# The first weight sum of a seven-product pair: from a VectorE addition to a GpSimd transfer that adds on writing

## The chip, the cores and the metric

One core of a Trainium2 chip runs the whole program. The metric is the device time of one execution in microseconds (us). The kernel before takes 2045.4 us, the median of 2 runs (2044.98 to 2045.83).

The engines are named as in the profile: PE is TensorE (matmuls), DVE is VectorE, ACT is ScalarE, POOL is GpSimd, and SP is SyncE, whose queue issues nearly all transfers from memory.

## The reference

A block of a streaming encoder on 256 rows of width 4096, all in float32. Cut to the parts whose weights matter here:

```
xn   = rms_norm(x, norm_in_g)
proj = xn @ w_in                      # 4096 x 14336: q, k, v, z_a, a_c, g_c, z_c
y_a  = rms_norm(chunked_attention(q, k, v, rel_table)) * silu(z_a)
y_c  = rms_norm(conv_module(a_c, g_c, ..., w_pw)) * silu(z_c)
h    = x + concat(y_a, y_c) @ w_out   # 4096 x 4096
gate = sigmoid(rms_norm(h) @ w_ple_gate + b_ple_gate)   # 4096 x 4096
out  = rms_norm(h + gate * (p @ w_ple))
```

Nearly all of the time is the product of 256 rows with these weights, which are read once from memory, about 400 MB.

## The kernel before, in words

**Exact products from two parts.** A float32 weight block `wt` is split into a high part `wh` (a cast on ACT, type fp32r) and a low part `wl = wt - wh` (a subtraction on DVE, `minus`, line 321). The activations are split in the same way beforehand. One block product then costs three matmuls: high by high, low by high and high by low.

**Units.** The inner dimension is cut into blocks of 128 rows and the weight columns into blocks of 512. A unit takes one pair of row blocks (`k0 = 2*pair`, `k1 = k0 + 1`) and two column blocks that lie `apart` columns from each other. Its weights are two tiles of 128 x 2 x 512 (512 KB each): `w0` holds the two column blocks of `k0`, `w1` those of `k1`. With the two halves of the 256 rows, a unit is a 2 x 2 by 2 x 2 block product:

- A *pair* unit does it with eight block products: 24 matmuls. It needs 2 casts and 2 subtractions `minus`.
- A *seven* unit (marked with `*` in the orders of lines 266 to 270) does it with seven, by Strassen's and Winograd's scheme: 21 matmuls. It needs sums of the weights in place of one product: first `w0[:,1] = w0[:,1] + w1[:,1]` (`plus`, line 485), then `w0[:,0] = w0[:,1] - w0[:,0]` (`less`, line 486), then `w1 = w1 - w0[:,0]` (`less`, line 490). The first sum is that of the second column block of `k0` and the second column block of `k1`. `w0` and `w1` are also split before they are overwritten, and their sums are split after. On DVE that makes, in this order: `l0` (half a tile), the `plus`, the first `less`, `l1`, the second `less`, `al`, `bl`. On ACT the casts are `h0` (half a tile), `h1`, `ah` (line 488), `bh` (line 491).
- A *one* unit takes two row blocks of a single column block, 12 matmuls, with one tile.

`mixed_product` (line 430) runs 16 units of the kinds pair and seven in a given order; `product` (line 329) runs one units. There are 117 seven units: in the products of the convolution's gate and of q and k (orders `early`), in the four gate products (`delayed` once, then `dense`), in the four output products (`late`, then `dense`), and in three products with `w_ple_gate` (`late`, then `steady`). `dense` reads `1 0* 3 2* 5 4* 6* 7 8* 9 10* 11 12* 14* 13 15`: mostly pair and seven in turn, twice two sevens side by side.

**What sets the order.** The orders above are written out by hand. `prepare` (line 274) takes the next unit of the plan ahead of its use: it asks for its tiles in the pool `wpool` (`WB = 5` tiles of 512 KB for loads, and five buffers each for the high and the low parts), issues the loads from SP's queue and the first casts. In a seven unit, `prepare` for the next unit is called after the cast `bh`; its `al` and `bl` follow after it. `chain` (line 97) ties the splits and sums of each engine in the order in which they are written; other work is placed between them by the scheduler. A load has to wait until the last reader of the tile five places earlier is done. In a steady row of pair and seven in turn, the first tile `w0` of a seven unit takes the place of the second tile of the pair unit before last, which its `minus` frees; the second tile `w1` takes the place of the `w0` of the seven unit before, which `al` frees.

**Queues.** POOL does next to nothing before the change: a few fills, the power that makes a reciprocal root (line 148), four fills of the attention bias (line 919), and four operations at the end. No transfer is issued from it.

Of the kernel before, what the change touches and what calls it, by code (L numbers as in the profile page):

```python
# [13 lines left out]
ALU = mybir.AluOpType  # L14
# [3 lines left out]
NB = 512  # L18
# [13 lines left out]
def hybrid_block(  # L32
# [23 lines left out]
    nc = tc.nc  # L56
# [40 lines left out]
    def chain(ins):  # L97

        prev = last_of.get(ins.ins.engine)
        if prev is not None:  # L100
            tc.add_manual_dep(
                ins.ins, prev.name,
                mybir.DependencyInfo(mybir.DependencyClass.NoSync, mybir.DependencyReason.DATA),
                reason="order of the parts",
            )
        last_of[ins.ins.engine] = ins.ins
        return ins
# [101 lines left out]
    def fill(n):  # L209
        step()  # L210
        credit[0] += n
        while later and credit[0] > 0:
            item = later.popleft()
            weight, item = item if isinstance(item, tuple) else (1, item)
            credit[0] -= weight
            item()
        if not later:
            credit[0] = 0
# [11 lines left out]
    def part(tag):  # L230
        return wpool.tile([P, KC, NB], F32R, tag=tag, name=tag, bufs=HB)
# [42 lines left out]
    def prepare():  # L274

        if prepared or not plan:
            return
        unit = plan.popleft()
        w, col, apart, at, kind = unit
        wts, highs = [], []  # L280
        if kind == "one":
            wt = wpool.tile([P, KC, NB], F32, tag="w", name="wt")
            nc.sync.dma_start(
                wt,
                w[at * P : (at + KC) * P, col : col + NB].rearrange("(k q) n -> q k n", q=P),
            )
            wts.append(wt)
        else:
            for k in range(2):
                wt = wpool.tile([P, 2, NB], F32, tag="w", name="wt")  # L290
                kb = 2 * at + k
                rows = w[kb * P : (kb + 1) * P, :]
                nc.sync.dma_start(
                    wt,
                    bass.AP(
                        tensor=rows.tensor, offset=rows.offset + col,
                        ap=[list(rows.ap[0]), [apart, 2], [1, NB]],
                    ),
                )
                wts.append(wt)  # L300
        for k, wt in enumerate(wts):
            n = 1 if kind == "seven" and k == 0 else 2
            highs.append(part("wh"))
            chain(nc.scalar.copy(highs[k][:, :n], wt[:, :n]))  # L304
        prepared.append((unit, wts, highs))

    def take(*unit):

        prepare()
        found, wts, highs = prepared.pop()  # L310
        assert found[1:] == unit[1:] and found[0] is unit[0], (found, unit)
        return wts, highs
# [7 lines left out]
    def minus(wl, wt, wh):  # L320
        return chain(nc.vector.tensor_tensor(wl, wt, wh.bitcast(F32), ALU.subtract))  # L321

    def plus(out, a, b):
        return chain(nc.vector.tensor_tensor(out, a, b, ALU.add))  # L324

    def less(out, a, b):
        return chain(nc.vector.tensor_tensor(out, a, b, ALU.subtract))  # L327
# [102 lines left out]
    def mixed_product(  # L430
        w, col, lhs, comb, order, on_helpers, ahead=None, fills=0, on_begin=None, apart=NB
# [13 lines left out]
        def add(name, x, w2, n, final):  # L445

            for kind, (a, b) in enumerate(((x[0], w2[0]), (x[1], w2[0]), (x[0], w2[1]))):
                made.append(
                    nc.tensor.matmul(  # L449
                        banks[name], a, b, start=name not in begun,  # L450
                        stop=final and ends[name] == n and kind == 2,
                    )
                )
                begun.add(name)

        def block(kb, h):
            t = lhs[kb // 4]
            return [t[:, kb % 4, q, h * P : (h + 1) * P] for q in range(2)]

        last_seven = max((n for n, (_, seven) in enumerate(order) if seven), default=None)  # L460
        for n, (pair, seven) in enumerate(order):
            if ahead:
                ahead(pair)
            (w0, w1), (h0, h1) = take(w, col, apart, pair, "seven" if seven else "pair")
            l0, l1 = part("wl"), part("wl")
            if not seven:
                for wt, wh, wl in ((w0, h0, l0), (w1, h1, l1)):
                    minus(wl, wt, wh)
                prepare()
                fill(fills[0] if isinstance(fills, tuple) else fills)  # L470
                parts = ((h0, l0), (h1, l1))
                places = [(k, j, h) for k in range(2) for j in range(2) for h in range(NH)]
                if n in (0, len(order) - 1):
                    places = [(k, j, h) for j in range(2) for h in range(NH) for k in range(2)]
                for k, j, h in places:
                    name = (("P2", "P3"), ("P4", "X"))[h][j]
                    add(name, block(2 * pair + k, h), [t[:, j] for t in parts[k]], n, k == 1)
                continue
            begins = not helper
            if begins:  # L480
                for name in ("P1", "P5", "P7", "P6"):
                    helper[name] = ps_tmp.tile([P, NB], F32, tag="tmp", name=f"acc_{name}")
                banks.update(helper)
            minus(l0[:, :1], w0[:, :1], h0[:, :1])
            plus(w0[:, 1], w0[:, 1], w1[:, 1])
            less(w0[:, 0], w0[:, 1], w0[:, 0])
            ah, bh = part("wh"), part("wh")
            chain(nc.scalar.copy(ah, w0))  # L488
            minus(l1, w1, h1)
            less(w1, w1, w0[:, :1].to_broadcast([P, 2, NB]))  # L490
            chain(nc.scalar.copy(bh, w1))  # L491
            prepare()
            fill(fills[1] if isinstance(fills, tuple) else fills)
            al, bl = part("wl"), part("wl")
            minus(al, w0, ah)
            minus(bl, w1, bh)
            first = len(made)

            def s_of(i):
                t, at = comb[pair // 4], pair % 4  # L500
                return [t[:, at + i // 2, q, (i % 2) * P : (i % 2 + 1) * P] for q in range(2)]

            k0, k1 = 2 * pair, 2 * pair + 1
            add("P1", block(k0, 0), (h0[:, 0], l0[:, 0]), n, True)
            add("P2", block(k1, 0), (h1[:, 0], l1[:, 0]), n, True)
            add("P3", s_of(3), (h1[:, 1], l1[:, 1]), n, True)
            add("P6", s_of(2), (ah[:, 0], al[:, 0]), n, True)
            add("P7", s_of(0), (ah[:, 1], al[:, 1]), n, True)
            add("P5", s_of(1), (bh[:, 1], bl[:, 1]), n, True)
            add("P4", block(k1, 1), (bh[:, 0], bl[:, 0]), n, True)  # L510
            if begins and on_begin:
                on_begin()
            if begins:
                tc.add_manual_dep(
                    made[first].ins, last_transpose[0].ins.name,
                    mybir.DependencyInfo(mybir.DependencyClass.NoSync, mybir.DependencyReason.DATA),
                    reason="transposes before the helpers take their banks",
                )
            if n == last_seven:
                on_helpers(helper)  # L520
# [74 lines left out]
    def first_products():  # L595
# [21 lines left out]
        def add(k, parts, *kinds):  # L617
# [13 lines left out]
    rows = [(conv_ln_g, KCW), (conv_ln_b, KCW), (b_dw, KCW), (attn_out_g, AW // P),  # L631
            (conv_out_g, KCW), (ple_norm_g, KD)]
# [360 lines left out]
    for c in range(6):  # L993
        rows = spool.tile([P, 2, NB], F32, tag="stage", name="comb")
# [76 lines left out]
    for c0 in range(0, D // NB, 2):  # L1071
# [8 lines left out]
        def on_helpers(helper):  # L1080
            _, z = sum_tiles()
            h00, h01, h10, h11 = (hs[c0 + j][:, h, :] for h in range(NH) for j in range(2))
            tt(h00, helper["P1"], h00, ALU.add)
            helper_sums(helper, z)
            tt(h01, h01, z[0][1], ALU.add)
            tt(h10, h10, z[1][0], ALU.add)
            tt(h11, h11, z[1][1], ALU.add)
# [150 lines left out]
```

## Time and profile before

| | |
|---|---|
| time, median of 2 runs | 2045.4 us (2044.98 to 2045.83) |
| the profiled execution's own time | 2045.17 us |
| its span, first to last instruction | 2043.4 us |
| PE busy | 2018.3 us (99%), 9103 matmuls |
| DVE busy | 1801.0 us (88%) |
| ACT busy | 1373.3 us (67%) |
| POOL busy | 14.7 us (1%) |
| transfers | 412.29 MB, 202 GB/s over the span |
| granted TensorE clock | 0.996 |

Busy time is a mean over stages that differ: the profile's 40 slices show DVE between half busy (the last ones) and nine tenths or more (the gate, output and ple-gate products). The chain of waits follows the work back from the last instruction to what released it, so it says which engine's work set the end. A group row gives the summed busy time of instructions of one line and kind, the mean duration in ns, and after the bar the idle time of that engine just ahead of them. A timeline row starts with its start and its duration in us; a row with `x5` holds five instructions one after the other. SPq rows are issues of transfers, whose landing is a different row: the transfers' view gives the time from issue to landing.

### The profile page before, as it was taken

What the parts mean: (1) busy time and instruction counts of PE and PEld (TensorE: products, weight loads), DVE (VectorE), ACT (ScalarE), POOL (GpSimd) and SP (SyncE); (2) the same over time, 40 slices, a digit from 0 to 9 for tenths busy, and PEclk for the clock granted to TensorE, in tenths of its full rate; (3) what the DMA queues carried; (4) which work ended last, traced back from release to release, by engine and by line L of the source; (5) the groups of instructions that cost most, each with busy time, mean ns of one, the idle gap of its engine ahead of it and who ended that gap; (6) DMA issues with size and microseconds to landing.
All of it is one profiled execution on the core that took longest, in us unless ns stands there. A gap on an engine that the chain in (4) does not pass through costs nothing.

```text
span 2043.4 us, 26018 instructions
## 1 busy us (share of the span) xinstructions
PE 2018.3 (99%) x9103; PEld 1668.4 (82%) x9103; DVE 1801.0 (88%) x2124; ACT 1373.3 (67%) x2033; POOL 14.7 (1%) x23
## 2 busy tenths in 40 slices
PE   9999999999999999999999999999999999999997
PEld 6888888888888888878888888888888888888886
DVE  7589997999799988975889999999999998999954
ACT  7477798778977797774555656675565675665543
POOL 0000000000000000000000000000000000000010
PEclk9999999999999999999999999999999999999999
DMA  8646665666566665746565665666656655666774
GB/s 303 186 165 207 191 208 171 213 195 208 165 198 203 196 196 175 217 153 214 171 227 173 214 208 192 239 227 198 214 191 221 206 191 191 211 229 206 230 221 144
DMA packets 170333, 412.29 MB, mean 202 GB/s; under 512 B 13006, under 2 KB 16222, under 8 KB 170202
## 3 DMA queue, kind: packets, MB, share of 16 engines
q1 hardware_dynamic: 169914, 410.11, 62.1%
q8 instruction: 71, 1.16, 0.2%
q10 hardware_dynamic: 288, 0.52, 0.1%
q14 instruction: 60, 0.49, 0.1%
HBM read 406.39 MB, written 4.19 MB: 201 GB/s over the span
## 4 chain that ended last, share of the span: by engine, by line
PE 95%; DVE 2%; ACT 1%; issue 1%; DMA 1%; ACTq 0%; POOLq 0%; POOL 0%; DVEq 0%
PE acc L449 55%; PE acc L255 22%; PE acc_P L449 15%; DVE wl L321 1%; PE tmp_ps L179 1%; DMA wt<-in_w_in_dram 0%; PE tmp_ps L888 0%; PE tmp_ps L924 0%; PE tmp_ps L946 0%; ACT big_t L854 0%; ACT wh L304 0%; ACT junk L564 0%; PE tmp_ps L134 0%; DMA pin<-in_p_dram 0%; PE tmp_ps L923 0%
## 5 line engine op out<-in xcount | busy, mean ns | idle before, releaser
L321 DVE TENSOR_TENSOR wl<-wt,wh 128x1024 fp32r<-128x1024 f32 x961 | 1091.8, 1156 | 143.0 <-ACT wh L304 119.4
L449 PE MATMUL acc<-wh,big_t 128*128 128x512 f32 x3410 | 1052.2, 390 | 1.3 <-ACT big_t L165 0.7
L304 ACT CAST wh<-wt 128x1024 fp32r<-128x1024 f32 x727 | 698.5, 981 | 324.1 <-PE acc L449 106.1
L449 PEld LDWEIGHTS acc<-wh,big_t 128*128 128x128 f32 x3410 | 638.4, 188 | 133.5 <-ACT big_t L165 1.2
L449 PE MATMUL acc<-wl,big_t 128*128 128x512 f32 x1705 | 662.8, 389 | 0.4 <-DVE wl L321 0.4
L255 PE MATMUL acc<-wh,big_t 128*128 128x512 f32 x1248 | 393.8, 397 | 7.1 <-ACT wh L304 5.7
L449 PEld LDWEIGHTS acc<-wl,big_t 128*128 128x128 f32 x1705 | 320.0, 188 | 67.5 <-DVE wl L321 0.8
L255 PEld LDWEIGHTS acc<-wh,big_t 128*128 128x128 f32 x1248 | 232.5, 189 | 55.8 <-ACT wh L304 6.5
L449 PE MATMUL acc_P<-wh,big_t 128*128 128x512 f32 x852 | 262.2, 389 | 0.3 <-ACT wh L491 0.3
L255 PE MATMUL acc<-wl,big_t 128*128 128x512 f32 x624 | 244.1, 392 | 0.1
L327 DVE TENSOR_TENSOR wt<-wt 128x512 f32<-128x512 f32 x234 | 224.2, 958 | 7.5
L491 ACT CAST wh<-wt 128x1024 fp32r<-128x1024 f32 x117 | 123.3, 1054 | 158.1 <-DVE wt L327 129.2
L716 ACT ACTIVATE prod<-uT,dw 128x255 f32<-128x255 f32 (+14 forms) x480 | 200.7, 489 | 2.7 <-DVE cv L723 2.5
L449 PEld LDWEIGHTS acc_P<-wh,big_t 128*128 128x128 f32 x852 | 159.7, 188 | 33.6 <-ACT wh L491 0.7
L488 ACT CAST wh<-wt 128x1024 fp32r<-128x1024 f32 x117 | 123.3, 1054 | 81.5 <-DVE wt L327 76.4
L449 PE MATMUL acc_P<-wl,big_t 128*128 128x512 f32 x426 | 165.3, 389 | 0.0
L723 DVE TENSOR_TENSOR cv<-cv,prod 128x1020 f32<-128x1020 f32 (+14 forms) x120 | 138.7, 1156 | 21.2 <-ACT prod L716 21.0
L255 PEld LDWEIGHTS acc<-wl,big_t 128*128 128x128 f32 x624 | 117.5, 189 | 26.5 <-DVE wl L321 1.3
L449 PEld LDWEIGHTS acc_P<-wl,big_t 128*128 128x128 f32 x426 | 79.9, 188 | 17.0 <-DVE wl L321 0.2
L324 DVE TENSOR_TENSOR wt<-wt 128x512 f32<-128x512 f32 x117 | 80.2, 685 | 0.2 <-DMA wt<-in_w_ple_gate_dram 0.2
L564 ACT ACTIVATE junk<-hc 128x512 bf16<-128x512 f32 x32 | 20.2, 630 | 20.9 <-DVE hc L1095 8.4
L165 ACT ACTIVATE big_t<-tmp_ps,prm 128x256 fp32r<-128x256 f32 x64 | 27.5, 473 | 4.6 <-DVE big_t L166 4.6
(190 smaller groups left out, 937.9 us busy)
## 6 DMA issues: line engine op xcount, KB each, us to landing
wt<-in_w_in_dram SPq DMA_DIRECT2D x447, 512.0 KB, 4.6
wt<-in_w_out_dram SPq DMA_DIRECT2D x128, 512.0 KB, 4.6
wt<-in_w_ple_gate_dram SPq DMA_DIRECT2D x128, 512.0 KB, 4.4
wt<-in_w_pw_dram SPq DMA_DIRECT2D x32, 512.0 KB, 4.6
hc<-in_x_dram SPq DMA_DIRECT2D x8, 512.0 KB, 5.4
wt<-in_w_ple_dram SPq DMA_DIRECT2D x8, 512.0 KB, 5.5
out_dram<-hc SPq DMA_DIRECT2D x16, 256.0 KB, 2.7
xin<-in_x_dram SPq DMA_DIRECT2D x7, 512.0 KB, 8.0
```

Of the source, the lines that this page charges most:

```text
L165: nc.scalar.activation(hi, src, AF.Identity, scale=scale),
L179: nc.tensor.transpose(pt[:, i * T + h * P : i * T + (h + 1) * P], src[:, h, b * P : (b + 1) * P], ident,)
L255: nc.tensor.matmul(acc, a, b[:, k, :], start=kb == 0 and kind == 0, stop=kb == kblocks - 1 and kind == 2,)
L304: chain(nc.scalar.copy(highs[k][:, :n], wt[:, :n]))
L321: return chain(nc.vector.tensor_tensor(wl, wt, wh.bitcast(F32), ALU.subtract))
L324: return chain(nc.vector.tensor_tensor(out, a, b, ALU.add))
L327: return chain(nc.vector.tensor_tensor(out, a, b, ALU.subtract))
L449: nc.tensor.matmul(banks[name], a, b, start=name not in begun, stop=final and ends[name] == n and kind == 2,)
L488: chain(nc.scalar.copy(ah, w0))
L491: chain(nc.scalar.copy(bh, w1))
L716: chain(nc.scalar.activation(dst[:, i, : T - n], uT[:, i, : T - n], AF.Identity, scale=dw[:, b, TAPS - 1 - n : TAPS - n], bias=0.0 if n el ...
L723: chain(nc.vector.tensor_tensor(cv[:, :, n:], cv[:, :, n:], made[n][:, :, : T - n], ALU.add))
```

## The change

In `prepare`, the two loads of a seven unit are followed by a third transfer, of 256 KB: it is issued from POOL's queue, reads the second column block of `k1` from memory once more (`rows` still names `k1` after the loop), and adds it to the second half of `w0` on writing. `w0[:,1]` so becomes the sum that `plus` made, and the `plus` in `mixed_product` goes. Nothing else is edited. Lines from 301 on move down by 4, those after 485 by 3: `minus` is line 325, `less` line 331.

```diff
--- before.py
+++ after.py
@@ -298,6 +298,10 @@
                     ),
                 )
                 wts.append(wt)
+            if kind == "seven":
+                nc.gpsimd.dma_start(
+                    wts[0][:, 1, :], rows[:, col + apart : col + apart + NB], accum_op=ALU.add
+                )
         for k, wt in enumerate(wts):
             n = 1 if kind == "seven" and k == 0 else 2
             highs.append(part("wh"))
@@ -482,7 +486,6 @@
                     helper[name] = ps_tmp.tile([P, NB], F32, tag="tmp", name=f"acc_{name}")
                 banks.update(helper)
             minus(l0[:, :1], w0[:, :1], h0[:, :1])
-            plus(w0[:, 1], w0[:, 1], w1[:, 1])
             less(w0[:, 0], w0[:, 1], w0[:, 0])
             ah, bh = part("wh"), part("wh")
             chain(nc.scalar.copy(ah, w0))
```

In the rows below, the names in brackets are what the instruction waits for: `DMAHW` counts the landings of SP's transfers, `DMASW` those of POOL's, and an engine's name its own counter.

DVE before, a seven unit of the fourth gate product (its unit `2*`), with the pair unit ahead of it:

```order
1141 L321 TENSOR_TENSOR wl<-wt,wh 128x1024 [waits DMAHW0_49,PE_49,Activation_49]
1142 L321 TENSOR_TENSOR wl<-wt,wh 128x1024 [waits DMAHW1_49,PE_49,Activation_49]
1143 L321 TENSOR_TENSOR wl<-wt,wh 128x512 [waits DMAHW2_49,PE_49,Activation_49]
1144 L324 TENSOR_TENSOR wt<-wt 128x512 [waits DMAHW3_49]
1145 L327 TENSOR_TENSOR wt<-wt 128x512 [waits DVE_49]
1146 L321 TENSOR_TENSOR wl<-wt,wh 128x1024 [waits PE_49,Activation_49]
1147 L327 TENSOR_TENSOR wt<-wt 128x1024 [waits DVE_49]
```

and the same unit on DVE after the change:

```order
1077 L325 TENSOR_TENSOR wl<-wt,wh 128x1024 [waits DMAHW0_49,PE_49,Activation_49]
1078 L325 TENSOR_TENSOR wl<-wt,wh 128x1024 [waits DMAHW1_49,PE_49,Activation_49]
1079 L325 TENSOR_TENSOR wl<-wt,wh 128x512 [waits DMAHW2_49,PE_49,Activation_49]
1080 L331 TENSOR_TENSOR wt<-wt 128x512 [waits DMASW0_49,DVE_49]
1081 L325 TENSOR_TENSOR wl<-wt,wh 128x1024 [waits DMAHW3_49,PE_49,Activation_49]
1082 L331 TENSOR_TENSOR wt<-wt 128x1024 [waits DVE_49]
```

The `plus` of line 324, which waited for the landing of `w1` (`DMAHW3`), is gone; the first `less` stands in its place and waits for POOL's transfer; the landing of `w1` is now waited for by `l1` (and by the cast `h1` on ACT, as before).

DVE before, at the start of the same product (lines 1051 and 216 are the end of the product before: 1051 empties its accumulators):

```order
1126 L1051 TENSOR_TENSOR z<-acc_10170,z 128x512 [waits PE_49]
1127 L321 TENSOR_TENSOR wl<-wt,wh 128x512 [waits DMAHW6_49,Activation_49]
1128 L1051 TENSOR_TENSOR z<-acc_10172,z 128x512 [waits DVE_49,PE_49]
1129 L216 SCALAR_TENSOR_TENSOR y_c<-y_c,r_c,z 128x512 [waits Activation_49,Pool_49]
1130 L324 TENSOR_TENSOR wt<-wt 128x512 [waits DMAHW7_49]
1131 L1051 TENSOR_TENSOR z<-acc_10171,z 128x512 [waits PE_49]
1132 L216 SCALAR_TENSOR_TENSOR y_c<-y_c,r_c,z 128x512 [waits Activation_49]
1133 L1051 TENSOR_TENSOR z<-acc_10173,z 128x512 [waits PE_49]
1134 L327 TENSOR_TENSOR wt<-wt 128x512 [waits DVE_49]
```

and after the change (line 1054 is the former 1051):

```order
1063 L325 TENSOR_TENSOR wl<-wt,wh 128x512 [waits DMAHW6_49,PE_49,Activation_49]
1064 L1054 TENSOR_TENSOR z<-acc_10170,z 128x512 [waits PE_49]
1065 L331 TENSOR_TENSOR wt<-wt 128x512 [waits DMASW7_49,DVE_49]
1066 L1054 TENSOR_TENSOR z<-acc_10172,z 128x512 [waits PE_49]
1067 L216 SCALAR_TENSOR_TENSOR y_c<-y_c,r_c,z 128x512 [waits Activation_49,Pool_49]
1068 L1054 TENSOR_TENSOR z<-acc_10171,z 128x512 [waits PE_49]
```

Here the first `less` has moved up: it stood behind all four emptyings of accumulators and now stands ahead of three of them.

POOL after the change, around the first gate product (before, the fill of line 922, then line 919, and the powers of line 148 follow each other there):

```order
57 L922 MEMSET bias 64x4x64 [waits DVE_49,DMAHW7_49,PE_49,Pool_49]
58 L148 TENSOR_TENSOR r_ln<-r_ln,mhalf 128x2 [waits DVE_49]
59 L148 TENSOR_TENSOR r_a<-r_a,mhalf 128x2 [waits DVE_49]
60 L302 DMA wt<-in_w_in_dram 128x512 [waits DMAHW3_49,DMAHW4_49,DMAHW2_49,DMAHW5_49,DMAHW0_49,DMAHW7_49,DMASW1_49,DVE_49]
61 L148 TENSOR_TENSOR r_c<-r_c,mhalf 128x2 [waits DVE_49]
62 L302 DMA wt<-in_w_in_dram 128x512 [waits DMAHW1_49,DMAHW0_49,DMAHW3_49,DMASW5_49,DMAHW6_49,DVE_49,Activation_49]
```

The 117 transfers stand in one row on POOL, with its few other instructions between them. Of the landings that each waits for, the youngest is that of its own `w0`; the others belong to tiles of earlier units. On SP's queue the order differs only around some loads of `x` in the first output product and one load of a bias row.

## The prediction

> **What bounds the kernel now.** I read the page's busy times and chain first, then the waits of PE, then the chain and the DVE rows inside a single seven unit.
>
> ```profile
> span 2043.4 us, 26018 instructions
> PE 2018.3 (99%) x9103; PEld 1668.4 (82%) x9103; DVE 1801.0 (88%) x2124; ACT 1373.3 (67%) x2033; POOL 14.7 (1%) x23
> ```
>
> ```profile
> PE 95%; DVE 2%; ACT 1%; issue 1%; DMA 1%; ACTq 0%; POOLq 0%; POOL 0%; DVEq 0%
> ```
>
> The first lines give the span and each engine's busy time, the last the chain's shares. PE is busy for 2018.3 of 2043.4 us and is 95% of the chain. What an engine beside it saves can come back only where PE waits for it, and PE's longest waits are these (us in total, times, longest):
>
> ```profile
> PE acc L255 <- ACT wh L304: 5.7, 2, 4.5
> ...
> PE acc L449 <- DVE wl L321: 0.4, 1, 0.4
> PE acc_P L449 <- ACT wh L491: 0.3, 1, 0.3
> ```
>
> Only the last two belong to seven units (line 449): 0.7 us. The 5.7 us belong to one units (line 255), which the change leaves alone. So the gain is at most about 0.7 us, and the question is what the new transfer can cost. For that the fourth gate product is read, first on the chain, in which the run of nine `acc_P` marks a seven unit:
>
> ```profile
> 1270.57 2.04 PE acc_P L449 x9
> ...
> 1275.33 2.04 PE acc_P L449 x9
> ...
> 1285.53 2.04 PE acc_P L449 x9
> ```
>
> PE runs without a gap: a pair and a seven in turn take 1285.53 - 1275.33 = 10.20 us (45 matmuls), two sevens side by side 1275.33 - 1270.57 = 4.76 us. These three runs are the units `4*`, `6*` and `8*`. DVE, for `6*`, `8*` and `10*`:
>
> ```profile
> 1269.65 0.69 DVE L324 TENSOR_TENSOR wt<-wt 128x512 f32<-128x512 f32 x1
> ...
> 1273.38 1.22 DVE L321 TENSOR_TENSOR wl<-wt,wh 128x1024 fp32r<-128x1024 f32 x1
> ...
> 1278.67 0.68 DVE L324 TENSOR_TENSOR wt<-wt 128x512 f32<-128x512 f32 x1
> 1279.39 0.69 DVE L327 TENSOR_TENSOR wt<-wt 128x512 f32<-128x512 f32 x1
> 1280.00 1.22 DVE L321 TENSOR_TENSOR wl<-wt,wh 128x1024 fp32r<-128x1024 f32 x1
> 1281.25 1.23 DVE L327 TENSOR_TENSOR wt<-wt 128x1024 f32<-128x1024 f32 x1
> 1282.39 2.50 DVE L321 TENSOR_TENSOR wl<-wt,wh 128x1024 fp32r<-128x1024 f32 x2
> ...
> 1287.69 0.69 DVE L324 TENSOR_TENSOR wt<-wt 128x512 f32<-128x512 f32 x1
> ```
>
> DVE needs 1287.69 - 1278.67 = 9.02 us for a pair and a seven, so it regains 10.20 - 9.02 = 1.18 us on PE in each. A seven alone costs it the half subtraction `l0`, 0.6, and 1278.67 to 1282.39 + 2.50, 6.2: 6.8 us, where PE, side by side with another seven, needs 4.76. So it uses up its lead there: `al` of `6*` ends at 1273.38 + 1.22 = 1274.60, and PE's run that reads it starts at 1275.33. DVE is less than 1 us ahead then, and a delay that returned with every seven unit would reach PE.
>
> **What is removed.** One `plus` per seven unit:
>
> ```profile
> L324 DVE TENSOR_TENSOR wt<-wt 128x512 f32<-128x512 f32 x117 | 80.2, 685 | 0.2 <-DMA wt<-in_w_ple_gate_dram 0.2
> ```
>
> 117 x 0.685 = 80.2 us of DVE; with its spacing in the rows above (1278.67 to 1279.39) 0.72 us per unit. On the path it is worth at most the 0.7 us of PE's waits. What takes its place as DVE's last wait is `l1`, which needs the cast `h1`, which needs `w1`:
>
> ```profile
> 1274.62 0.33 SPq L293 DMA_DIRECT2D wt<-in_w_in_dram  x1
> wt<-in_w_in_dram SPq DMA_DIRECT2D x1, 512.0 KB, 3.8
> 1278.57 1.05 ACT L304 CAST wh<-wt 128x1024 fp32r<-128x1024 f32 x1 [1.54 <-DMA wt<-in_w_in_dram]
> ```
>
> The load of `8*`'s `w1` goes out when `al` of `6*` ends, lands 3.8 us later, and is cast until 1279.62; `l1` starts at 1280.00. Without the `plus`, `l1` moves forward by 0.38 us, not by 0.72.
>
> **What is added.** A chain: `w0` lands, POOL issues, 256 KB are read and added, the first `less` starts. POOL's queue is idle and the other landings that it waits for are older, so the chain starts at the landing of `w0`. How long it may last without moving `less` is the time from there to the `plus` of today. Two units, each with the issue of `w0`, its time to landing, and its `plus` (that of `10*` is above):
>
> ```profile
> 1278.18 0.33 SPq L293 DMA_DIRECT2D wt<-in_w_in_dram  x1
> wt<-in_w_in_dram SPq DMA_DIRECT2D x1, 512.0 KB, 5.6
> 455.48 0.37 SPq L293 DMA_DIRECT2D wt<-in_w_in_dram  x1
> wt<-in_w_in_dram SPq DMA_DIRECT2D x1, 512.0 KB, 5.8
> 467.21 0.69 DVE L324 TENSOR_TENSOR wt<-wt 128x512 f32<-128x512 f32 x1
> ```
>
> `10*`: 1278.18 + 5.6 = 1283.8, and 1287.69 - 1283.8 leaves 3.9 us. In an `early` product: 455.48 + 5.8 = 461.3, and 467.21 leaves 5.9 us. Each has 0.7 us more before DVE is later than today, since the `plus` is gone.
>
> The transfer itself, from POOL's issue to its landing, is not in this trace; no row has a transfer that adds, nor one issued from POOL. The nearest are the plain ones of 256 KB that SP issues among the weight loads, and the shortest (one of 256 KB) and longest landing of any weight tile:
>
> ```profile
> row<-in_b_ple_gate_dram SPq DMA_DIRECT2D x8, 256.0 KB, 4.9
> DMA to landing us min/median/max: 3.0/4.6/9.7
> ```
>
> So it lies between 3.0 and 9.7 us. I take 5.0: it runs among weight loads as the 4.9 us row does, and it reads as many bytes as a 512 KB load (256 KB from memory, 256 KB of the old values), which takes 4.6. With 5.0 us the early products hide it (5.9), and `10*` starts `less` at 1288.8 instead of 1288.41, a delay of 0.4 us that the next pair regains.
>
> The Trainium skill ("DMA: Bandwidth & Descriptors", section "Anatomy of one DMA — SWDGE (gpsimd) path") fits transfers from GpSimd by 2.0 us plus bytes over 436 GB/s; worked out for 256 KB that is an estimate of 2.6 us, by which all units hide it and the sum would be 2045 us. It names no price for the adding, and no run here shows one yet.
>
> **The load beside it.** The new transfer moves its data while `w1` is under way, and `w1` is what DVE waits for next. The engines' share of one load:
>
> ```profile
> q1 hardware_dynamic: 169914, 410.11, 62.1%
> ```
>
> 0.621 x 2043.4 us for 410.11 MB is 1.62 us for a 512 KB tile on all 16 engines, 0.81 us for 256 KB. A `w1` that shares the engines lands later by 0.8 us, or 1.6 if the old values cost as much as the new ones; below nothing it can't go, as nothing is removed from any queue. From one issue of `w1` to the next, today: 3.8 + 0.1 + 1.05 (cast), then `l1`, `less`, `al` from 1280.00 to 1283.61, 3.6 us: 8.6 us. It becomes 9.4 to 10.2, against DVE's 9.02 of today and PE's 10.20. In turns DVE keeps up, but regains only 0 to 0.8 us. A `dense` product has two sevens that follow a seven; each costs 6.8 - 4.76 = 2.0 us of lead today, 1.3 without the `plus`, 2.6 us per product, to be regained in five turns. I take 1.0 us of delay, nearer to the plain transfer's: five turns give 5 x 0.6 = 3.0, nothing is lost. At 1.6 us nothing is regained, and the six `dense` products (three of the gate, three of the output) lose 6 x 2.6 = 16 us.
>
> **Product starts.** In `dense` and `steady` products `less` now stands ahead of three emptyings of the last product's accumulators. If it waits, PE's banks wait. There the room is small:
>
> ```profile
> 1232.22 0.33 SPq L293 DMA_DIRECT2D wt<-in_w_in_dram  x1
> wt<-in_w_in_dram SPq DMA_DIRECT2D x1, 512.0 KB, 5.2
> 1240.24 0.69 DVE L1051 TENSOR_TENSOR z<-acc,z 128x512 f32<-128x512 f32 x1
> ```
>
> `w0` lands at 1237.4, the sum at 1242.4, and the emptying of 1240.24 comes 2.2 us late. It is the second bank of four; PE fills the first for six matmuls, 6 x 10.20 / 45 = 1.4 us, before it needs the next. That is between nothing and 0.8 us for each of eight starts, up to 6 us; I take 2. POOL's `r_c` now queues behind a transfer, but it is wanted only in the third gate product.
>
> **Sum.** The profiled execution took 2045.17 us for its span of 2043.4, 0.2 below the median. 2045.2 - 0.7 + 2 = 2046.5, with the median's 0.2 us 2046.7; I forecast 2047.
>
> **The rivals.** *The sum comes late* (slower). If adding costs more than I take, `less` waits in every seven unit. This feeds back: the split of pair unit 7, ahead of `8*`, frees the place for the `w0` of `10*`, and two turns later the split of pair unit 11, behind `10*`, frees that of another seven. In between lie 5.6 us of load, the transfer, and DVE's work from a `less` to the end of the next pair's split, 1279.39 to 1287.69 less the `l0` of 0.6, 7.7 us. Two turns of PE are 20.4 us, so it decides from a transfer of 20.4 - 13.3 = 7.1 us. At 8 us each turn costs 0.45 us, 117 x 0.45 = 53, and eight starts another 8 x 3 = 24: 2122. At the bound of 9.7, 117 x 1.3 + 40 = 192: 2237. For it: no row shows the price of adding, and bytes are read twice. Against: the rows of 256 KB stay below 5.
>
> *DVE locks POOL out* (slower still). If POOL can prepare its transfer only while DVE stands still, it begins only when DVE stops at the `less` that waits for it. DVE in this stretch (the third busy time), and POOL's fills of the bias:
>
> ```profile
> 1278.67:1287.69 9.02, 9.02 (x42) 7.46 (x41) 8.89 (x11) 5.63 (x7) 0.00 (x0) 1.00 0.67 234
> L919 POOL MEMSET bias<- x4: 304/305/307, 286.4 to 859.6; 64x256 f32 x4
> ```
>
> DVE is busy 8.89 of 9.02 us: no gap to begin in. Each seven unit would stand for the 5.0 us, less the 0.7 of the `plus` and about 1 us of lead: 117 x 3.3 = 386, 2431 us. Against it: the four fills, beside a working DVE, took 304 to 307 ns, none longer, so POOL's own writes were not held up. The Trainium skill ("SBUF — State Buffer", section "Who interferes with whom") says that a GpSimd transfer can be starved, as its descriptors are written through ports that VectorE shares, by VectorE's modes that use both pairs of ports; and that a `tensor_tensor` with two inputs in SBUF takes only the read side, which descriptors don't need (inferred there). No run here shows yet which of the two holds for a transfer.
>
> *The loads crowd* (no change): 1.6 us of delay and late starts, 2045 + 16 + 6 = 2067, still within 2%. *All is hidden* (no change): a transfer of 3 us, 2044.7. *It doesn't do what it says*: the order of instructions shows 117 transfers for 117 additions, so this has no chance worth a number.
>
> **How the numbers follow.** About 2% (41 us) is what a measurement of this kernel can tell from no change. Forecast 0.50, crowding 0.14, all hidden 0.09: 0.73 within 2%. The late sum 0.21 and the lockout 0.05: 0.26 slower. Faster by 2% would need 41 us where PE waits for 0.7: 0.01. The range reaches from 2040 (all hidden, with the one units' waits shrinking too) to 2130, which takes in the late sum up to 8 us; beyond lie the lockout and half of the late sum, about 0.16. The forecast's own range is 2043 to 2058.
>
> **What would show it.** Right: the group of line 324 gone; `less` (line 331) with waits for POOL's transfer of under 1 us in the dense products and none in the early ones; a time from POOL's issue to landing near 5.0; idle time of DVE ahead of `l1` that grows; PE still 99% busy. Wrong: POOL's transfers landing after 7 us, `less` on the chain, or PE below 97%. If loads from SP take over 6 us in the median, crowding is what I underrated.

## The result, and the profile after

The changed kernel takes 2111.69 us, the median of 2 runs (2110.9 to 2112.48), against 2045.4 before: a ratio of 1.0324, 95% interval 1.0299 to 1.0348. It is 66 us slower. The profiled execution has a span of 2109.1 us.

The page of the changed kernel: span and busy times, transfer queues (packets, MB, share of 16 engines), the chain's shares, the `less` and POOL's transfer, and the time from issue to landing of the loads and of POOL's transfers:

```profile
span 2109.1 us, 26583 instructions
...
PE 2040.7 (97%) x9103; PEld 1665.7 (79%) x9103; DVE 1728.2 (82%) x2007; ACT 1359.5 (64%) x2033; POOL 116.0 (5%) x140
...
q1 hardware_dynamic: 169914, 410.11, 58.7%
q0 software_dynamic: 16848, 30.68, 9.1%
...
PE 69%; DMA 13%; DVE 10%; issue 5%; ACT 3%; DVEq 0%; ACTq 0%; POOLq 0%; POOL 0%
...
L331 DVE TENSOR_TENSOR wt<-wt 128x512 f32<-128x512 f32 x234 | 224.3, 959 | 144.9 <-DMA wt<-in_w_in_dram 78.4
...
L302 POOL DMA_DIRECT2D wt<-in_w_in_dram x71 | 62.0, 874 | 1048.5 <-DMA wt<-in_w_in_dram 431.4
...
wt<-in_w_in_dram SPq DMA_DIRECT2D x447, 512.0 KB, 5.0
wt<-in_w_out_dram SPq DMA_DIRECT2D x128, 512.0 KB, 5.1
...
wt<-in_w_in_dram POOLq DMA_DIRECT2D x71, 256.0 KB, 5.7
...
wt<-in_w_out_dram POOLq DMA_DIRECT2D x28, 256.0 KB, 4.7
wt<-in_w_ple_gate_dram POOLq DMA_DIRECT2D x18, 256.0 KB, 6.0
```

DVE is busy for 1801.0 - 1728.2 = 73 us less, as the `plus` went, and got 145 us of idle time ahead of `less` in return, nearly all of it waiting for a transfer. PE fell from 99% to 97%, and on the chain from 95% to 69%: transfers (13%) and DVE (10%) have taken most of its place. The busy share hides a part of the loss: PE's busy time grew from 2018.3 to 2040.7 us with the same 9103 matmuls, so of the 66 us 43 are time without a matmul and 22 lie in what the profile counts as busy. The granted clock is one part of that: 0.994 in this execution and 0.992 in that of run e11, against 0.996 before. Worked out over the spans, that is an estimate of about 4 to 5 and 8 to 9 us of TensorE's time; whether the waits brought the lower clock about was not tested.

The waits of the changed kernel (us in total, times, longest) show both ends of the loss:

```profile
DVE wl L325 <- ACT wh L308: 121.9, 118, 2.0
...
DVE wt L331 <- DMA wt<-in_w_in_dram: 78.4, 34, 6.0
...
DVE wt L331 <- DMA wt<-in_w_out_dram: 37.8, 10, 4.8
...
DVE wt L331 <- DMA wt<-in_w_ple_gate_dram: 23.0, 8, 4.5
...
PE acc_P L453 <- DVE wl L325: 17.9, 26, 0.8
```

`less` waited 78.4 + 37.8 + 23.0 = 139 us in 52 of 117 units for POOL's sums. PE's waits in seven units, 0.4 and 0.3 us before, are now 17.9 us in 26 for `acc_P` alone, all for DVE. One unit shows how: `10*` of the fourth gate product, which the prediction worked through. Its `w0` goes out at 1308.27 and lands 5.9 us later; these rows of the changed kernel's timeline are SP's loads from then on, POOL's transfer and the `less`:

```profile
1308.27 10.30 SPq L293 DMA_DIRECT2D wt<-in_w_in_dram  x5
...
1314.95 0.87 POOL L302 DMA_DIRECT2D wt<-in_w_in_dram  x1 [9.20 <-DVE wl L325]
...
1321.88 0.69 DVE L331 TENSOR_TENSOR wt<-wt 128x512 f32<-128x512 f32 x1 [3.06 <-DMA wt<-in_w_in_dram]
```

The view of the transfers for the 0.3 us around POOL's issue, with the time to landing at the end of each row:

```profile
wt<-in_w_in_dram SPq DMA_DIRECT2D x1, 512.0 KB, 4.4
wt<-in_w_in_dram POOLq DMA_DIRECT2D x1, 256.0 KB, 6.8
```

The load landed at 1314.2 (1308.27 + 5.9), POOL issued at 1314.95, the sum landed 6.8 us later, and `less` had then stood for 3.06 us. Of the five loads in the first row one is `w0`; the other four went out at 1314.69, 1315.98, 1317.11 and 1318.25, the first of them 0.26 us ahead of POOL's.

Over the 112 seven units for which the trace has all the landings, the sum came 6.3 us after `w0` in the median, 4.6 at the least, 7.5 at the upper quarter, 9.2 at most. 0.7 us of it lies between the landing of `w0` and POOL's issue. From that issue, the landing follows the loads around it: with no load or other transfer issued by SP between 2 us before and 1 us after POOL's issue (35 of the 117 transfers) it took 4.2 us in the median, with one (51) 5.7, with two (28) 7.2.

By products: the time from the second `less` of a product's first seven unit to that of the next product, or to the end, in the changed kernel less the same before, summed over each kind. A second profiled execution of the same kernel, from run e11, stands beside it; what is left to the difference of the spans (about 1 us) lies ahead of the first product. Between these two executions of one kernel the share of a kind differs by up to 8 us, so only the large differences in the table can be read.

| products | transfers | lost, us | lost, us (e11) |
|---|---|---|---|
| early (convolution gate, q and k) | 42 | 8.5 | 14.4 |
| first gate product (`delayed`) | 5 | 2.9 | 2.3 |
| `dense` and `steady` | 62 | 57.6 | 50.0 |
| `late` | 8 | -2.0 | -1.0 |

### The profile page after: what moved, and what is told of

It is laid out like the page before. It is cut to its first block, busy times and chain, and to the rows that moved or that the text cites. A ratio compares the mean times of both kernels' runs of the same rounds, so it can differ in the third digit from the quotient of the medians.

```text
span 2109.1 us, 26583 instructions
## 1 busy us (share of the span) xinstructions
PE 2040.7 (97%) x9103; PEld 1665.7 (79%) x9103; DVE 1728.2 (82%) x2007; ACT 1359.5 (64%) x2033; POOL 116.0 (5%) x140
## 3 DMA queue, kind: packets, MB, share of 16 engines
q0 software_dynamic: 16848, 30.68, 9.1%
## 4 chain that ended last, share of the span: by engine, by line
PE 69%; DMA 13%; DVE 10%; issue 5%; ACT 3%; DVEq 0%; ACTq 0%; POOLq 0%; POOL 0%
PE acc L453 37%; PE acc L255 21%; PE acc_P L453 9%; DMA wt<-in_w_in_dram 7%; DVE wl L325 7%; DMA wt<-in_w_out_dram 4%; DMA wt<-in_w_ple_gate_dram 1%; DVE wt L331 1%; ACT wh L494 1%; PE tmp_ps L179 1%; ACT wh L308 1%; PE tmp_ps L927 0%; PE tmp_ps L891 0%; DVE cv L726 0%; PE tmp_ps L949 0%
## 5 line engine op out<-in xcount | busy, mean ns | idle before, releaser
L331 DVE TENSOR_TENSOR wt<-wt 128x512 f32<-128x512 f32 x234 | 224.3, 959 | 144.9 <-DMA wt<-in_w_in_dram 78.4
L494 ACT CAST wh<-wt 128x1024 fp32r<-128x1024 f32 x117 | 123.1, 1052 | 148.4 <-DVE wt L331 107.7
L302 POOL DMA_DIRECT2D wt<-in_w_in_dram x71 | 62.0, 874 | 1048.5 <-DMA wt<-in_w_in_dram 431.4
L302 POOL DMA_DIRECT2D wt<-in_w_out_dram x28 | 24.4, 871 | 336.6 <-DVE wt L331 94.5
```

The costliest lines, as they stand in the source:

```text
L302: nc.gpsimd.dma_start(wts[0][:, 1, :], rows[:, col + apart : col + apart + NB], accum_op=ALU.add)
```

## The experiments

The theory after the result was the prediction's first rival: the sum comes late, `less` waits, and the wait returns through the places for tiles (A). Against it stood: the loads are crowded by the added bytes (B); POOL is held up by DVE; the order at the product starts. Diffs are against the changed kernel, unless said otherwise; `...` stands for lines left out.

**e1, no first sum at all.** What is the removal worth without its replacement?

```diff
-            if kind == "seven":
-                nc.gpsimd.dma_start(
-                    wts[0][:, 1, :], rows[:, col + apart : col + apart + NB], accum_op=ALU.add
-                )
```

> The first weight sum is left out altogether: neither VectorE's addition nor the transfer (the first `less` reads the unsummed block, in the same place of the order as in the changed kernel). If the 66 us come from the transfer, in whatever way, this takes 2044 to 2046 us: only the 0.7 us that PE waited for in seven units can come back. If they come from the new order at the product starts (the first `less` ahead of three emptyings of accumulators), this takes up to 2050 us.

Measured: 2044.76 us, ratio to before 0.9998 (0.9988 to 1.0007). DVE did 1733.2 us of work in place of 1801.0, and the kernel gained nothing by it: DVE's subtractions waited for ACT's casts of line 304 instead. Before, and in this run:

```profile
DVE wl L321 <- ACT wh L304: 119.4, 111, 2.1
...
DVE wl L321 <- ACT wh L304: 169.0, 163, 2.1
```

Instruction by instruction in the trace, 148.4 of the 169.0 us stand ahead of the splits of pair and one units (108.1 before), 17.3 ahead of `l0` (11.3) and only 3.2 ahead of `l1` (none before). A version that still has to make the sum can hardly be faster than that, and the new order at the starts costs nothing by itself.

**e2, the transfer that nobody waits for.** DVE's addition is back; POOL first reads one column of `w0`, so that its transfer is released by the same landing, and adds into a spare tile. (The extra read puts its issue 1.3 us behind that landing in the median, in place of 0.7.)

```diff
             if kind == "seven":
...
+                nc.gpsimd.tensor_copy(spare[:, :1], wts[0][:, 1, :1])
                 nc.gpsimd.dma_start(
-                    wts[0][:, 1, :], rows[:, col + apart : col + apart + NB], accum_op=ALU.add
+                    spare, rows[:, col + apart : col + apart + NB], accum_op=ALU.add
                 )
...
+            plus(w0[:, 1], w0[:, 1], w1[:, 1])
             less(w0[:, 0], w0[:, 1], w0[:, 0])
```

> VectorE's addition stays, and the same 117 adding transfers of 256 KB are issued from GpSimd at the same places, at the landing of w0, but into a spare tile that nobody reads. Theory A, the sum comes late and `less` waits for it: nothing waits here, 2045 to 2055 us, and PE's 99% are back. Theory B, the transfers' bytes delay the loads beside them: the loss stays, 2090 to 2115 us, and the loads' median stays at 5.0 us or more.

Measured: 2047.34 us, ratio 1.0010 (1.0001 to 1.0020). The page of this run:

```profile
PE 2020.3 (99%) x9103; PEld 1669.6 (82%) x9103; DVE 1801.7 (88%) x2124; ACT 1372.0 (67%) x2033; POOL 226.1 (11%) x258
...
spare<-in_w_in_dram POOLq DMA_DIRECT2D x71, 256.0 KB, 6.3
```

The transfers were there, as long as in the changed kernel or longer, and cost 2.3 us. The loads were slowed as in the changed kernel, too (median 4.9 us out of `w_in` and 5.2 out of `w_out`; 4.6 each before, 5.0 and 5.1 in the changed kernel). So the bytes are not the loss (B falls); the wait for the sum is.

**e3, the transfer without the adding.** It overwrites the block, so the first sum is left out here as in e1.

```diff
-                    wts[0][:, 1, :], rows[:, col + apart : col + apart + NB], accum_op=ALU.add
+                    wts[0][:, 1, :], rows[:, col + apart : col + apart + NB]
```

> The same transfer in the same place and with the same waits, but it overwrites the second block of w0 instead of adding to it (the sum is left out of the computation). If the adding is what makes the transfer long, the time from issue to landing falls from 5.6 to about 4 us in the median, from 7 to 8 to about 5 us behind a load, and the kernel takes 2045 to 2060 us. If it is the place behind a load in the transfer engines, whatever is moved, the landing stays above 5 us and the kernel stays at 2085 to 2110 us.

Measured: 2053.7 us, ratio 1.0044 (1.0030 to 1.0058). The page is that of its longest execution, 2061.06 us:

```profile
q0 software_dynamic: 9360, 30.68, 4.9%
...
L331 DVE TENSOR_TENSOR wt<-wt 128x512 f32<-128x512 f32 x234 | 224.1, 958 | 78.6 <-DMA wt<-in_w_in_dram 34.4
...
L302 POOL DMA_DIRECT2D wt<-in_w_in_dram x71 | 38.5, 542 | 1041.1 <-DMA wt<-in_w_in_dram 455.4
...
wt<-in_w_in_dram POOLq DMA_DIRECT2D x71, 256.0 KB, 4.0
```

The same bytes by the count took 4.9% of the engines in place of 9.1%, POOL 0.54 us in place of 0.87, and a landing came 4.0 us after the issue in place of 5.7 (transfers out of `w_in`). Of the 66 us, 8 to 9 are left (16 in the profiled execution). So the adding makes most of the loss; a transfer at this place isn't free even without it.

**e4, `l1` ahead of the first `less`.**

```diff
             minus(l0[:, :1], w0[:, :1], h0[:, :1])
+            minus(l1, w1, h1)
             less(w0[:, 0], w0[:, 1], w0[:, 0])
             ah, bh = part("wh"), part("wh")
             chain(nc.scalar.copy(ah, w0))
-            minus(l1, w1, h1)
```

> Changed kernel with the order of two steps exchanged on VectorE: the subtraction l1 (1.2 us) before the first `less`, so the sum may come 1.2 us later. Theory A: of the 141 us that `less` stood idle, the 43 waits above 1.25 us have 80 us in excess of it, so at most 80 us of waiting stay and, as the loop of two turns also gains 1.2 us, 2055 to 2085 us. Theory B: the loads come as late as before, 2100 to 2112 us.

Measured: 2085.44 us, ratio 1.0197 (1.0178 to 1.0217), 0.4 us beyond the range that A gave. The waits of this run:

```profile
DVE wl L325 <- ACT wh L308: 183.2, 168, 2.6
...
DVE wt L331 <- DMA wt<-in_w_in_dram: 20.2, 15, 3.8
DVE wt L331 <- DMA wt<-in_w_out_dram: 18.1, 10, 3.1
...
DVE wt L331 <- DMA wt<-in_w_ple_gate_dram: 12.8, 6, 3.1
```

`less` waited 51 us in place of 139, but the subtractions waited 183 for casts, 61 more than in the changed kernel; `l1`, now first, has 63 of it, 17 in the changed kernel. What A had not counted: while `less` waited for the sum, the cast of `w1` was being made. The wait partly changed its place.

**e5, six places for weight tiles in place of five.**

```diff
-WB = 5
+WB = 6
```

> Changed kernel with six places for weight tiles instead of five, so each load may be issued one tile's use earlier. Theory A: the loop from a freed place over load, transfer and `less` to the next freed place has one place more, the sum is there in time also at 7 to 8 us: 2044 to 2052 us, waits of `less` under 20 us in total. Theory B: the same bytes meet the same loads, 2090 to 2112 us.

Measured: 2050.8 us, ratio 1.0029 (1.0017 to 1.0041). The page:

```profile
PE 2019.2 (99%) x9103; PEld 1666.9 (81%) x9103; DVE 1729.9 (84%) x2007; ACT 1370.4 (67%) x2033; POOL 117.2 (6%) x140
...
L331 DVE TENSOR_TENSOR wt<-wt 128x512 f32<-128x512 f32 x234 | 224.2, 958 | 57.1 <-DMA wt<-in_w_in_dram 24.7
```

The same 117 transfers with the same adding, and 60 of the 66 us are gone. In the `dense` and `steady` products the sums came hardly earlier after `w0` (6.0 us in the median and 7.1 at the upper quarter, 6.3 and 7.9 with five places); in the early ones they did (4.9 in place of 6.3). What changed for all of them is that each load goes out one tile earlier. `less` waited longer than the under 20 us that A expected, and yet PE hardly did: a late sum costs little as long as the next load doesn't hang on it. That is what the loop through the places says, and with one place more the loss is nearly gone.

**e6 and e12, the first seven unit of each dense and steady product summed by VectorE.** `by_hand` holds these 8 units.

```diff
-            if kind == "seven":
+            if kind == "seven" and (id(w), col, at) not in by_hand:
...
+            if (id(w), col, pair) in by_hand:
+                plus(w0[:, 1], w0[:, 1], w1[:, 1])
             less(w0[:, 0], w0[:, 1], w0[:, 0])
```

> Changed kernel, but the first seven unit of each dense and steady product (8 of the 117) has VectorE's addition again and no transfer. In the trace of the changed kernel these `less` waited 2.9, 6.0 and 5.4 us in the gate products and not at all in the output products, so if the waits at the starts reach PE, about 14 us go away, up to 20 with what they delay: 2092 to 2100 us. If the loss is made in turns inside the products, as the output products' growth from one seven unit to the next suggests, 2105 to 2112 us.

Measured: 2104.39 us, ratio 1.0298 (1.0279 to 1.0317), between the two ranges that were expected, with an interval that overlaps the changed kernel's. So it was run again with the changed kernel beside it.

> The changed kernel itself, beside the other two for an interval in the same job: 2108 to 2114 us.

> The first seven unit of each dense and steady product summed by VectorE again, now against the changed kernel in the same job: alone and with six places, this edit took off 7.3 us and 2.9 us, each with intervals that overlap. If the waits at the starts reach PE, it is 5 to 9 us below the changed kernel here with intervals apart; if not, within 3 us of it.

Measured: the changed kernel (e11) 2110.64 us, ratio 1.0323 (1.0308 to 1.0337); the starts by hand (e12) 2110.31 us, ratio 1.0316 (1.0302 to 1.0330). The edit is worth nothing that can be told; the 7 us of e6 did not come back. At least in part they go along with the granted clock: the two runs of e6 at 0.996 took 2102.4 and 2102.8 us, its two at 0.994 2106.0 and 2110.5, and the runs of e11 and e12 had 0.991 to 0.994. In the waits of e11's profile PE stood for an emptying at a start in two instances:

```profile
PE acc L453 <- DVE z L1054: 7.7, 2, 4.3
```

and in those of e12's for `acc_P`, as it does inside the products:

```profile
PE acc_P L455 <- DVE wl L327: 21.8, 32, 0.7
```

In e12 the wait for the emptying at a start is no longer among PE's waits, but those for `acc_P` in seven units have grown, 21.8 us in place of e11's 16.7, and by products the `dense` and `steady` ones lose the same, 49.5 us in place of 50.0. So what is saved at a start seems to be lost again in the turns that follow; with one profiled execution each, and 8 us between two of the changed kernel, that is not shown.

**e9, six places and the starts by hand.** The two edits together.

> Six places for weight tiles, and the first seven unit of each dense and steady product summed by VectorE again (8 of 117). The run with six places alone still lost 5.7 us, of which its trace places 2 to 3 us at each of the gate products that follow another. If what is left there is the wait of the first `less`, ahead of the emptyings, 2045 to 2048 us. If it is spread over the units, 2049 to 2052 us. It can't be faster than the 2044.8 us of the kernel without any first sum.

Measured: 2047.94 us, ratio 1.0013 (1.0003 to 1.0023). It is the nearest to the kernel before, but its interval overlaps that of e5 (1.0017 to 1.0041), so what the starts cost with six places stays open.

**e7 and e8, the transfers by themselves.** Behind the last output of the kernel before, POOL issues 256 KB transfers one at a time, each waiting for all that was issued with the one before; `load` is a 512 KB load from SP, the first of them issued 0.1 to 0.3 us ahead of POOL's transfer, or 0.1 us behind it in the kind with four loads and a busy VectorE. The diff is that of e8; e7 has one load at most.

```diff
+            for k, t in enumerate(loads[:n_loads]):
+                nc.sync.dma_start(t, ...)
+            if kind.endswith("dve"):
+                nc.vector.tensor_copy(work[:, 0, :1], mark)
+                for _ in range(8):
+                    nc.vector.tensor_tensor(work, src, work, ALU.subtract)
+            nc.gpsimd.dma_start(
+                dst[:, 1, :], block, **({"accum_op": ALU.add} if kind.startswith("adds") else {})
+            )
```

> Kernel before with a tail behind its last output (its time is longer by the tail and says nothing): 256 KB transfers from GpSimd one at a time, four each: plain; adding; adding with a 512 KB load from SP issued at the same moment; plain with such a load; adding beside a VectorE busy with subtractions of 128x1024. If adding itself is dear, the second kind takes 5 us or more; if a load in front is what makes it long, the second kind takes about 4 us and the third 6.5 to 8 us, and the load too lands late; if VectorE holds GpSimd up, GpSimd's 0.87 us per issue grow in the fifth kind and fall below that in the second.

> Kernel before with another tail behind its last output (its time says nothing). Four times each: a 512 KB load from SP alone; the adding transfer of 256 KB with 2 such loads issued back to back, the first just before it; the adding one with 4; a plain one with 4; the adding one with 4 and with 1, VectorE busy with subtractions of 128x1024 beside it. One load cost the adding transfer only 0.5 us in the tail before (4.2 to 4.7 us), inside the kernel it takes 6.5 to 8.4 us. If the queue of several loads makes the rest, the adding transfer takes 6.5 us or more with 4 loads, 5 to 6 with 2, and a plain one with 4 loads gains over 1 us on it; if VectorE's work makes it, the last two kinds are over 1 us longer than the same without VectorE.

Measured, the transfers' view over one kind after the other (median us from issue to landing of four). In e7: plain; adding; adding with one load (ahead of it the row of the loads, with one of the next kind); plain with one load; adding beside a busy VectorE:

```profile
t<-in_w_in_dram POOLq DMA_DIRECT2D x4, 256.0 KB, 2.9
...
t<-in_w_in_dram POOLq DMA_DIRECT2D x4, 256.0 KB, 4.2
...
t<-in_w_in_dram SPq DMA_DIRECT2D x5, 512.0 KB, 3.7
t<-in_w_in_dram POOLq DMA_DIRECT2D x4, 256.0 KB, 4.7
...
t<-in_w_in_dram POOLq DMA_DIRECT2D x4, 256.0 KB, 4.1
...
t<-in_w_in_dram POOLq DMA_DIRECT2D x4, 256.0 KB, 4.2
```

In e8: a load alone; adding with two loads; adding with four; plain with four; adding with four and with one beside a busy VectorE:

```profile
t<-in_w_in_dram SPq DMA_DIRECT2D x4, 512.0 KB, 3.4
...
t<-in_w_in_dram POOLq DMA_DIRECT2D x4, 256.0 KB, 6.4
...
t<-in_w_in_dram POOLq DMA_DIRECT2D x4, 256.0 KB, 7.5
...
t<-in_w_in_dram POOLq DMA_DIRECT2D x4, 256.0 KB, 5.1
...
t<-in_w_in_dram POOLq DMA_DIRECT2D x4, 256.0 KB, 6.9
...
t<-in_w_in_dram POOLq DMA_DIRECT2D x4, 256.0 KB, 4.8
```

Adding costs 1.3 us with nothing else under way (4.2 against 2.9), 0.6 with one load (4.7 against 4.1) and 2.4 with four (7.5 against 5.1). One load beside it costs the adding transfer 0.5 us (4.7, where e7 expected 6.5 to 8 if a load in front were the reason); two cost 2.2, four 3.3. No cost of VectorE's work shows (4.2 with it and 4.2 without, with one load 4.8 and 4.7; the 6.9 and 7.5 with four loads compare less well, as the order of issue differs). `10*` above, with four loads of which the first went out 0.26 us ahead, took 6.8.

**e10, all 62 seven units of the dense and steady products summed by VectorE.** The diff is that of e6, with all units of those orders in `by_hand`.

> Changed kernel, but all 62 seven units of the dense and steady products are summed by VectorE again; the transfer stays in the 55 others (42 in the early products, 13 in the delayed and late ones). From the start of one product to that of the next, the trace of the changed kernel loses 8 us in the seven early products together, 3 in the first gate product, 58 in the eight dense and steady ones, and gains 2 in the late ones. If the loss is made where the places for tiles are tight, this takes 2045 to 2057 us. If each of the 117 transfers costs about the same, 55 of 117 of the loss stay: 2076 us.

Measured: 2063.36 us, ratio 1.0091 (1.0078 to 1.0105), between the two cases that were expected. By products, its profiled execution loses 2.3 us in the dense and steady ones, and 12.0 in the early ones. If the two parts simply add up, the 62 transfers there cost 2110.6 - 2063.4 = 47 us, 0.76 each, and the other 55 cost 18.5, 0.34 each. The transfers outside the dense and steady products are cheaper, but they are not hidden. (The profiled execution's span is 2057.6 us, 14 more than before, so its products add up to less than the 18.5 us of the medians.)

## Why the prediction went as it did

The time, 2111.7, lies in the range of 2040 to 2130 only because that took in the case that was given 0.21; the forecast of 2047 missed it by 65 us, and its mechanism, that the transfer is hidden, did not hold. Step by step:

- **PE bounds, at most 0.7 us to gain.** Right: e1 gained 0.3 us, within its interval of nothing. (Line 449 is that of the pair units too, and it had 1.3 us more of waits for `big_t`, which the shown rows leave out; the change touches neither.) **`l1` becomes the next wait.** Hardly so: without any sum (e1) `l1` waited 3.2 us in 10 of 117 units, and the time that DVE saved stood mostly ahead of the splits of pair and one units. In the changed kernel `l1` did wait, 17 us in 21 units, but the wait that counted was that of `less`, one step earlier.
- **The transfer, "I take 5.0".** This is the step that failed. It was added to the landing of `w0` to give that of the sum. From POOL's issue to its landing the transfer took 5.6 us in the median, and from the landing of `w0` 6.3. Three things were missing in it: the 0.7 us from a landing to POOL's issue; the adding, which was priced by its bytes as a load of 512 KB, and costs 1.3 us alone and 2.4 among four loads; and the spread. Where POOL's issue falls among the next loads changes from turn to turn, so one unit gets under 5 us and the next 8 (4.2 us from POOL's issue with no load around it, 7.2 with two, and e8 shows the same by itself); the 7.1 us at which the loop was said to decide lie below the upper quarter of 7.5. A median under the break-even was taken for safety, where 23 of the 62 units in the dense and steady products lie above it.
- **"The early products hide it (5.9)".** Wrong for the same reason: there too the median was 6.3, `less` waited in 19 of 42 units, up to 5.2 us, and e10 puts 18.5 us on the units outside the dense and steady products.
- **The rival "the sum comes late".** Right in its mechanism and near in its size (2122 at 8 us). The wait is the cause (e2), the adding makes its length (e3), and a sixth place undoes the loop (e5). Its sum was put together wrongly, though: 24 us of it were to come from the eight starts, and e12 shows nothing there (0.3 us); 53 us from all 117 units alike, where 62 of them carry 47 us. At the 6.3 us that the median unit took, the same sum gives no loss at all, as it has no spread in it; that it came near is in part luck. Against this rival stood that the rows of 256 KB stay below 5 us; one of `x` took 5.3 before the change (`xin`, in the transfers' view).
- **Product starts, 2 us.** The waits came about (7.7 us on PE, two instances), but taking them away gained nothing that can be told (e12).
- **Crowding, 16 us at most.** The bytes were sized rightly: 9.1% of 2109.1 us over 117 is 1.64 us of all engines per transfer, the upper of the two bounds. The price was not: 2.3 us in all (e2) against the 6 x 2.6 = 16 of this rival. A load of 3.4 us alone landed 3.7 us after its issue beside an adding transfer (e7's loads), and the loads' median inside the kernel rose from 4.6 to 5.0 and 5.1, under the 6 us that the prediction named as the sign.
- **DVE locks POOL out.** Excluded for this work of DVE: POOL's issue took 0.87 us in the kernel, 0.87 to 0.89 beside the busy VectorE of e7 and 0.86 to 0.91 without. The reading that the Trainium skill offers ("SBUF — State Buffer", section "Who interferes with whom"), that a `tensor_tensor` of two inputs leaves descriptors alone, agrees with this.
- The fit of the Trainium skill ("DMA: Bandwidth & Descriptors", section "Anatomy of one DMA — SWDGE (gpsimd) path"), 2.6 us as an estimate, is near the plain transfer with nothing else under way, 2.9 us. The 4.2 to 7.5 us that the adding one took in e7 and e8 are not what it speaks of.

A bookkeeping of DVE, set beside what the same profiled execution lost, fits two of four. In the changed kernel the waits of `less` (139) and the growth of those for casts (2.5), less the `plus` saved (80), come to 62 us, with 66 lost; in e4 51 + 64 - 80 = 35, with 36 lost. In e3 73 + 14 - 80 = 7, with 16 lost, and in e5 50 + 21 - 80 is negative, with 6 lost. So where this sum is small it doesn't give the loss. PE bounds there, and single waits of DVE can reach PE although DVE as a whole has time over; that is a likely reason and was not tested. What was not tried is a transfer that always goes out ahead of the next loads, so how much of the 6.3 us such an order would take off stays open. No version here is faster than the kernel before beyond its interval.

## What to carry to other kernels

Work taken from an engine that nobody waits for was worth nothing here (0.3 us in e1), and what replaces it must be judged by its latency on the path to the next buffer: from the landing of what it needs, over the issue, the transfer and its queue, to the first reader. Compare the spread of that latency, not its median alone, with the break-even of the buffer loop (here the upper quarter, 7.5 us, lay above the 7.1 and the median, 6.3, below); a place more for tiles did more here (60 of 66 us) than any change of order. And don't read a gain off one unpaired run of a kernel whose times spread: 7 us vanished when both kernels were run side by side, and the granted clock beside each run told part of it.

## What the runs showed of the hardware

- A transfer from GpSimd that adds on writing costs the transfer engines nearly twice the plain one: 9.1% of 2109.1 us against 4.9% of 2059.3 for the same 30.68 MB by the count, 1.64 against 0.86 us each, with 16848 packets against 9360. The count of bytes is the same for both, so it doesn't show this cost. GpSimd itself spends 0.87 us on the issue, against 0.54.
- Its landing depends on the loads issued around it: 4.2 us with none, 4.7 with one, 6.4 with two, 7.5 with four, where four loads brought a plain transfer from 2.9 to 5.1. In the changed kernel it was 4.2, 5.7 and 7.2 with none, one and two.
- It was not slowed by a VectorE at work on `tensor_tensor` with two float32 inputs (4.2 us with and without).
